# Where the per-layer input p is turned and split: in the expert stage's two ends, or during the input projection

## The chip, the core and the metric

The kernel runs on one core of a Trainium2 chip. The metric is device time in microseconds (us) for one launch, and the number to compare is the median of several launches. One further launch is recorded by the hardware profiler; its rows are what the text below rests on. The engines are PE (TensorE, matrix products and its weight loads PEld), DVE (VectorE), ACT (ScalarE), POOL (GpSimd) and SP (SyncE, which here only issues transfers). Each engine works through its own list of instructions in order, and waits at the head of the list for what the instruction needs.

## What is computed

The reference is a transformer-like encoder layer on 2048 tokens of width 1024, in f32. Cut to what matters here:

```
x   = layernorm(x)
z   = x @ w_in + b_in                      # 1024 -> 2048, then short convolutions and pooling
x   = layernorm(alpha * x + mix(z) @ w_o)
ffn = top-2 experts of 32 (SwiGLU, 1024 -> 512 -> 1024), weighted and summed per token
ple = sigmoid(x @ w_ple_gate + b) * (p @ w_ple_proj)     # p: 2048 x 256
out = layernorm(alpha * x + ffn + ple)
```

The `ple` line is called the embedding below. `p` is an input of 2048 rows by 256; nothing that is computed changes it.

## The kernel before

Products in f32 are made from two halves: a value is split into a high part (a rounding copy on ACT, line 304) and a low part (the difference, on DVE, line 305), and `mm3` (lines 219 to 221) adds high by high, high by low and low by high, each a 128x512 matrix product. An operand whose rows are tokens is first turned on PE (four or eight 128x128 products with the identity into PSUM) and then split out of PSUM.

On-chip memory is handed out in slots by the program as it is written: `FB` holds split operands (26 slots of 128x1024, 12 more before the expert stage), `RB` raw data (9 slots, 12 more from the expert stage on), `ZB` small tiles, `PS` the eight PSUM banks. `Slots.get` takes the slot that has been free longest, and `wait(slots, keep=k)` lets a background job step aside until k more than it needs are free. A background job is a generator that a main loop advances a step at a time (`start(name, gen, rate)`, `run`, `bg.step`). From the program so written a planner orders each engine's list once, when the kernel is built; the transfers that SP issues are in one such list, those of ACT and POOL in the lists of these engines.

The stages, with their times in the profile:

- Up to about 405 us, the input projection: two sweeps `s` over half of the tokens, four column groups `j`, two chunks `c` of 512 tokens (`unit`, 96 products of 128x512 each). Beside it run jobs that load and split the next weights, that rewrite the normalised input (`again`), and, from unit (1, 3, 3) on, `load_wo`, which loads and splits `w_o` (loads at line 596). From unit (1, 0, 3) on one RB slot of zeros is also stored to the unused rows of `yd` from POOL (line 653).
- To about 606 us, the output projection, layer norm and router (`wo_tiles`, `post`, `router`).
- To about 725 us, the embedding of tiles 10 to 15 (`PRE`, `embed`), with the routing beside it; then a loop for overflowing experts (line 1524).
- To about 1452 us, the experts (`stage1`, `stage2`, `hidden`; lines 1403 and 1404 are products for half blocks). Their results are stored to `yd`.
- To the end, the embedding of tiles 0 to 9 (`END`, `embed_tile`), while `finish` and `finish_last` gather each token's two expert rows from `yd` on POOL (line 1616), add them on DVE (lines 1653, 1630), normalise (ACT 1661 and 1667, POOL 1659 to 1669, DVE 1668), and store.

`p` enters only in the embedding. Two tiles at a time, `fetch_p` (line 1092) has SP load 256 rows into half an RB slot, and `load_p` turns them with four PE products (line 1125) into a PSUM bank and splits them into one FB slot, high parts in its first half and low parts in its second. There are eight such pairs: three in `PRE` and five in `END`. `embed_product` takes its left operands from that slot. `prepare` and `prepare_tile` start these jobs one or two tiles ahead, and `start_fetch` loads the first three pairs of `END` early and reserves the RB slots for it (`rclaims`).

In `embed_tile` the sums of the large product leave PSUM by DVE (line 1231, twice for each tile), ACT makes the tanh (1232), and DVE multiplies by the p product (1236).

Of the kernel before, what the change touches and what calls it, by code (L numbers as in the profile page):

```python
# [8 lines left out]
F32 = mybir.dt.float32  # L9
F32R = mybir.dt.float32r  # L10
# [6 lines left out]
N = 2048  # L17
D = 1024
KD = D // 128
NT = N // 128  # L20
# [151 lines left out]
def wait(slots, m=1, align=1, keep=0, late=False):  # L172
    n = 0
    while len(slots.age) < m + keep or not slots.has(m, align, late):
        n += 1
        assert n < 10000, "no slot"
        yield
# [3 lines left out]
def hybrid_conv_pool_hmoe_encoder(ctx, tc, x, p, ln0_g, ln0_b, w_in, b_in, conv_w, pool_w, pool_scale,  # L181
                                  w_o, ln1_g, ln1_b, w_rg, b_rg, w_re, b_re, w1, w3, w2, w_pg, b_pg,
                                  w_pp, ln2_g, ln2_b, out):
    nc = tc.nc
# [3 lines left out]
    FB, RB = Parts(), Parts()  # L188
# [6 lines left out]
    PS = psum.tile([128, 8, 512], F32, name="PS")  # L195
    SF, SR, SZ, SP = Slots(NF, NY), Slots(NR), Slots(NZ), Slots(8)

    def dram(name, shape):
        return nc.dram_tensor(name, shape, F32, kind="Internal").ap()
# [3 lines left out]
    x1d = dram("x1d", (N, D))  # L203
    x1Td = dram("x1Td", (len(END), 2, 128, 1024))
    yd = dram("yd", ((NB + NOV) * 128, D))

    def flat(ap, *shape):
        step, dims = 1, []
        for s in reversed(shape):
            dims.insert(0, [step, s])  # L210
            step *= s
        return bass.AP(tensor=ap.tensor, offset=ap.offset, ap=dims)
# [14 lines left out]
    ident = consts.tile([128, 128], F32, name="ident")  # L227
# [17 lines left out]
    for g in range(4):  # L245
        w = 2 << g
        l, r = w // 2, w // 2 - 1
# [12 lines left out]
    def run(gen):  # L260
        for _ in gen:
            bg.step()

    def after(n, gen):
        for _ in range(n):
            yield
        yield from gen
# [3 lines left out]
    def start(name, gen, rate):  # L271
        jobs[name] = gen
        bg.add(gen, rate)

    def need(name):

        if name in jobs:
            gen = jobs.pop(name)
            n = 0
            while next(gen, DONE) is not DONE:  # L280
                n += 1
                if n > 40:
                    bg.step()
            bg.forget(gen)
# [18 lines left out]
    def split(hi, lo, src, eng=nc.vector):  # L303
        nc.scalar.copy(hi, src)  # L304
        eng.tensor_sub(lo, src, hi)  # L305
# [75 lines left out]
    def again():  # L381

        gr0.append(SR.get())
        gr0.append(SR.get())
        nc.scalar.dma_start(RB[:, gr0[0]], bcast(ln0_g, D))
        nc.scalar.dma_start(RB[:, gr0[1]], bcast(ln0_b, D))
        for t in range(AGAIN):
            yield from wait(SR, keep=2)
            r = SR.get()
            nc.sync.dma_start(RB[:, r], xf[t * 128:(t + 1) * 128, :])  # L390
            yield
            v = RB[:, r]
            s = ln_stats(v)
            yield
            ln_apply(v, s, RB[:, gr0[0]], RB[:, gr0[1]])
            nc.gpsimd.dma_start(x0d[t * 128:(t + 1) * 128, :], v)
            SR.free(r)
            yield
# [21 lines left out]
    def load_w(s, j):  # L420

        for i in range(4):
            if (s, j, i) not in raw:
                yield from wait(SR)
                fetch_w(s, j, i)
                yield
            yield from wait(SF)
            hi = SF.get()
            yield from wait(SF)
            lo = SF.get()  # L430
            r = raw.pop((s, j, i))
            split(FB[:, hi], FB[:, lo], RB[:, r])
            SR.free(r)
            wz[s, j, i] = (hi, lo)
            yield
# [115 lines left out]
    b = SP.get()  # L551
# [20 lines left out]
    def load_wo():  # L572
# [44 lines left out]
        SF.free(ph)  # L617
        SF.free(pl)

    zero_rows = list(range(HROW + HCUM[NE] * 64, (NB + NOV) * 128, 128))  # L620
    for s in range(2):
        for j in range(4):
            for c in (2 * s, 2 * s + 1):
                if (s, j, c) == (0, 0, 0):
                    start("x1", prep(1), 0.8)
                if (s, j, c) == (0, 1, 0):
                    start("again", again(), 0.3)
                    start("x2", prep(2), 0.4)
                if (s, j, c) == (0, 3, 1):
                    start("x3", prep(3), 0.6)  # L630
                if (s, j, c) != (0, 0, 0):
                    need(f"x{c}")
                    need(f"w{s}{j}")
                if (s, j, c) == (1, 3, 2):
                    SF.limit = NF
                if (s, j, c) == (1, 0, 3):
                    need("again")
                    for q in gr0:
                        SR.free(q)
                    zr = SR.get()  # L640
                    nc.gpsimd.memset(RB[:, zr], 0.0)
                if c == 2 * s + 1:
                    if (s, j) == (1, 3):
                        start("wo", load_wo(), 0.75)
                    else:
                        nj = (s, j + 1) if j < 3 else (s + 1, 0)
                        start("w%d%d" % nj, after(9, load_w(*nj)), 0.75)
                run(unit(s, j, c))
                if s and j + c >= 3 and j < 3:
                    for _ in range(-(-len(zero_rows) // (8 - 2 * j - c))):  # L650
                        a = zero_rows.pop(0)
                        e = min(a + 128, (NB + NOV) * 128)
                        tc.keep_in_program_order(nc.gpsimd.dma_start(yd[a:e], RB[:e - a, zr]))
                if j == 3:
                    SF.free(xT[c][0], 4)
                    SF.free(xT[c][1], 4)
# [11 lines left out]
    v = RB[:, wrr, :KD * 36].rearrange("p (k e) -> p k e", e=36)  # L668
# [338 lines left out]


    w1f, w3f, w2f = flat(w1, NE, D, 512), flat(w3, NE, D, 512), flat(w2, NE, 512, D)
    wpg, wpp, pf = flat(w_pg, D, D), flat(w_pp, 256, D), flat(p, N, 256)  # L1010
    wt = {}
    raws = deque()

# [46 lines left out]
    claims, rclaims = [0], [0]  # L1060
    rkeep, routed = [3], []

    def claimed(n):
        yield from wait(SF, keep=n - 1)
        claims[0] -= n
        return [SF.get() for _ in range(n)]
# [18 lines left out]


    based = dram("based", (N, D))
    base, xs, pT, praw = {}, {}, {}, {}

    def fetch_p(ts):  # L1090
        praw[ts[0]] = SR.get()
        nc.sync.dma_start(RB[:, praw[ts[0]], :512].rearrange("p (q c) -> p q c", c=256),
                          pf[ts[0] * 128:(ts[1] + 1) * 128, :].rearrange("(q p) c -> p q c", p=128))

    def fetch_x1(t):
        base[t] = SR.get()
        nc.sync.dma_start(RB[:, base[t]], x1d[t * 128:(t + 1) * 128, :])

    def fetch_embed(ts):
        for i, t in enumerate(ts):  # L1100
            yield from wait(SR)
            rclaims[0] -= 1
            fetch_x1(t)
            if i % 2 == 0:
                yield from wait(SR)
                rclaims[0] -= 1
                fetch_p(ts[i:i + 2])
            yield

    def start_fetch(ts):  # L1110
        rclaims[0] += len(ts) + (len(ts) + 1) // 2
        start(f"fetch{ts[0]}", fetch_embed(ts), 1.0)

    def load_p(ts):

        if ts[0] not in praw:
            yield from wait(SR)
            fetch_p(ts)
            for _ in range(6):
                yield  # L1120
        r = praw.pop(ts[0])
        yield from wait(SP)
        b = SP.get()
        for k in range(4):
            nc.tensor.transpose(PS[:, b, k * 128:(k + 1) * 128], RB[:, r, k * 128:(k + 1) * 128], ident)
        SR.free(r)
        yield
        q, = yield from claimed(1)
        split(FB[:, q, :512], FB[:, q, 512:], PS[:, b])
        SP.free(b)  # L1130
        for i, t in enumerate(ts):
            pT[t] = (q, 2 * i)
        yield
# [14 lines left out]
    def prepare(ts):  # L1148
        for i in range(0, len(ts), 2):
            claims[0] += 1  # L1150
            start(f"p{ts[i]}", load_p(ts[i:i + 2]), 1.0)
        rclaims[0] += sum(t not in base for t in ts)
        start(f"x{ts[0]}", (v for t in ts for v in load_x1(t, False)), 1.0)
# [109 lines left out]
    for ts in groups:  # L1263
# [9 lines left out]
        c, q = divmod(ts[-1], 4)  # L1273
# [250 lines left out]
    with tc.For_i(0, nov_n, 1) as it:  # L1524
# [5 lines left out]
        b = SP.get()  # L1530
        for q in range(2 * NT):
            i, t = divmod(q, NT)
            v = ZB[:, z, (q % 4) * 128:(q % 4) * 128 + 128]
# [49 lines left out]
    def prepare_tile(i):  # L1583
        if i < len(END):
            t = END[i]
            if i % 2 == 0:
                claims[0] += 1
                start(f"p{t}", load_p(END[i:i + 2]), 1.0)
            claims[0] += 2
            start(f"x{t}", load_x1(t, True), 1.0)  # L1590

    start_fetch(END[:6])
    bg.step()
    claims[0] -= 3
# [128 lines left out]
```

## Time and profile before

| | us |
|---|---|
| three launches | 1624.75, 1619.27, 1623.60 |
| their median | 1623.6 |
| profiled execution, as a launch is timed | 1621.81 |
| its span in the profile | 1620.2 |
| mean granted TensorE clock in it | 0.988 of full speed |

The profile's page lists for each engine how long it was busy, and the same in 40 slices of the span. Its views are the groups of instructions by line, what each engine waited for, the instructions in order of time, the sums over chosen stretches, and the chain of waits followed back from the last instruction. A time in brackets behind an instruction is how long its engine had been idle, and the arrow names what ended that. L1125 is line 1125 of the kernel before.

### The profile page before, as it was taken

Reading aid. Unit: us, or ns where it says so; the run is one execution under the profiler, and the core shown is the slowest. Engines: PE = TensorE matmul, PEld = TensorE weight load, DVE = VectorE, ACT = ScalarE, POOL = GpSimd, SP = SyncE. Lnnn points to the kernel's source line nnn. Section 1 sums busy time; section 2 is a strip of 40 time slices with the busy share of each in tenths; the row PEclk is TensorE's granted clock in tenths of the full one; section 3 lists DMA queues with packets and bytes.
Section 4 is the critical chain, followed back from the end, with each engine's and each line's share of the span. In section 5 each row is a group of like instructions: output and inputs, shape, how many; then the busy total and the mean of one; then the engine's idle time right before and its main releaser. Section 6 shows DMA issues by size and latency. Waiting matters only on the chain.

```text
span 1620.2 us, 21581 instructions
## 1 busy us (share of the span) xinstructions
PE 1569.1 (97%) x7371; PEld 1291.6 (80%) x7371; DVE 1157.8 (71%) x1406; ACT 792.0 (49%) x940; POOL 478.3 (30%) x626
## 2 busy tenths in 40 slices
PE   6999999999999998999999999999999999999986
PEld 5887878887888887778888888888888888888865
DVE  7777574345566767768888788777888767776887
ACT  7343342113111124147777767776777657662342
POOL 3454262443233225010202121111212101006874
PEclk9999999999999999999999999999999999999988
DMA  6546168865376536369898998998898987998971
GB/s 209 182 162 214 65 205 276 305 252 161 122 255 205 174 126 253 120 236 383 315 373 314 362 350 309 355 358 330 328 360 302 355 279 274 362 331 332 340 265 65
DMA packets 204809, 427.88 MB, mean 264 GB/s; under 512 B 18856, under 2 KB 70616, under 8 KB 204696
## 3 DMA queue, kind: packets, MB, share of 16 engines
q1 hardware_dynamic: 162096, 292.33, 51.7%
q0 software_dynamic: 34080, 122.96, 20.5%
q10 hardware_dynamic: 8520, 11.18, 2.1%
q8 instruction: 59, 0.97, 0.2%
q14 instruction: 54, 0.44, 0.1%
HBM read 333.10 MB, written 93.32 MB: 263 GB/s over the span
## 4 chain that ended last, share of the span: by engine, by line
PE 37%; issue 11%; POOL 5%; DVE 1%; ACT 1%; DMA 0%; POOLq 0%; DVEq 0%; ACTq 0%
PE PS L219 9%; PE PS L221 9%; PE PS L220 9%; PE PS L1403 3%; PE PS L1404 3%; PE PS L311 2%; POOL RY L1616 1%; PE PS L1461 1%; DMA yd<-RB 0%; POOL RB L1616 0%; DVE RB L1653 0%; POOL RY L1669 0%; POOL rstd L1664 0%; PE PS L1331 0%; POOL nbias L1659 0%
## 5 line engine op out<-in xcount | busy, mean ns | idle before, releaser
L220 PE MATMUL PS<-FB 128*128 128x512 f32 (+1 forms) x1516 | 589.7, 389 | 5.0 <-DVE FB L305 5.0
L219 PE MATMUL PS<-FB 128*128 128x512 f32 (+1 forms) x1436 | 559.9, 391 | 11.6 <-DVE FB L305 7.0
L221 PE MATMUL PS<-FB 128*128 128x512 f32 (+1 forms) x1436 | 557.6, 389 | 1.8 <-DVE FB L305 1.8
L220 PEld LDWEIGHTS PS<-FB 128*128 128x128 f32 x1516 | 287.6, 190 | 61.5 <-DVE FB L305 5.7
L219 PEld LDWEIGHTS PS<-FB 128*128 128x128 f32 x1436 | 272.3, 190 | 66.9 <-DVE FB L305 7.9
L305 DVE TENSOR_TENSOR FB<-RY,FB 128x1024 fp32r<-128x1024 f32 x232 | 281.1, 1230 | 52.1 <-ACT FB L304 29.7
L221 PEld LDWEIGHTS PS<-FB 128*128 128x128 f32 x1436 | 272.0, 189 | 56.6 <-DVE FB L305 2.2
L305 DVE TENSOR_TENSOR FB<-RB,FB 128x1024 fp32r<-128x1024 f32 x212 | 257.5, 1228 | 79.0 <-ACT FB L304 67.3
L304 ACT CAST FB<-RB 128x1024 fp32r<-128x1024 f32 x216 | 223.7, 1050 | 148.5 <-PE PS L220 49.8
L304 ACT CAST FB<-RY 128x1024 fp32r<-128x1024 f32 x236 | 243.1, 1049 | 92.7 <-PE PS L220 27.0
L1316 POOL DMA_INDIRECT RY<-x1d,TBI x29 | 56.5, 1947 | 391.6 <-DVE FB L305 232.0
L305 DVE TENSOR_TENSOR FB<-PS,FB 128x1024 fp32r<-128x1024 f32 (+1 forms) x116 | 103.2, 898 | 68.5 <-ACT FB L304 68.3
L304 ACT CAST FB<-PS 128x1024 fp32r<-128x1024 f32 (+1 forms) x116 | 86.3, 758 | 115.8 <-PE PS L311 77.1
L220 PE MATMUL PS<-FB,FY 128*128 128x512 f32 x264 | 104.2, 395 | 0.0
L1403 PE MATMUL PS<-FB 128*128 128x512 f32 x264 | 103.8, 393 | 0.0
L1404 PE MATMUL PS<-FB 128*128 128x512 f32 x264 | 103.3, 391 | 0.0
L219 PE MATMUL PS<-FB,FY 128*128 128x512 f32 x216 | 86.0, 398 | 0.0
L221 PE MATMUL PS<-FB,FY 128*128 128x512 f32 x216 | 85.5, 396 | 0.0
L219 PE MATMUL PS<-FY,FB 128*128 128x512 f32 x180 | 71.9, 399 | 0.0
L221 PE MATMUL PS<-FY,FB 128*128 128x512 f32 x180 | 70.7, 394 | 0.0
L296 POOL TENSOR_SCALAR rstd<-mv 128x1 f32<-128x1 f32 x42 | 29.3, 700 | 137.2 <-DVE mv L291 124.3
L304 ACT CAST FY<-RB 128x1024 fp32r<-128x1024 f32 (+1 forms) x30 | 31.0, 1036 | 78.8 <-PE PS L220 59.8
(276 smaller groups left out, 2007.6 us busy)
## 6 DMA issues: line engine op xcount, KB each, us to landing
RY<-in_w_dram SPq DMA_DIRECT2D x224, 512.0 KB
RB<-in_w_dram SPq DMA_DIRECT2D x160, 512.0 KB
yd<-RB POOLq DMA_DIRECT2D x59, 512.0 KB
RB<-in_w_in_dram SPq DMA_DIRECT2D x32, 512.0 KB
RB<-in_x_dram SPq DMA_DIRECT2D x24, 512.0 KB
yd<-RY POOLq DMA_DIRECT2D x23, 512.0 KB
x1Td<-FB POOLq DMA_DIRECT2D x20, 512.0 KB
FB<-x1Td SPq DMA_DIRECT2D x20, 512.0 KB
```

The costliest lines, as they stand in the source:

```text
L219: nc.tensor.matmul(o, ah, bh, start=start, stop=False)
L220: nc.tensor.matmul(o, ah, bl, start=False, stop=False)
L221: nc.tensor.matmul(o, al, bh, start=False, stop=stop)
L296: nc.gpsimd.tensor_scalar(rstd[:, s:s + 1], mv[:, s, 1:2], EPS, None, op0=OP.add)
L304: nc.scalar.copy(hi, src)
L305: eng.tensor_sub(lo, src, hi)
L311: nc.tensor.transpose(v[:, k], src[:, k * 128:(k + 1) * 128], ident)
L1316: nc.gpsimd.indirect_dma_start(out=RB[0:64 if half else 128, rows[n]], out_offset=None, in_=x1d, in_offset=bass.IndirectOffsetOnAxis(ap=id ...
L1403: nc.tensor.matmul(o, xs[0][:, c], wh, start=start, stop=False)
L1404: nc.tensor.matmul(o, xs[0][:, c], wl, start=False, stop=stop)
L1461: nc.tensor.transpose(v[:, k], g[:, k * 128:(k + 1) * 128], ident[0:m, 0:m])
L1616: nc.gpsimd.indirect_dma_start(out=RB[:, yq[t, i]], out_offset=None, in_=yd, in_offset=bass.IndirectOffsetOnAxis(ap=SLI[:, i, t:t + 1], ax ...
```

## The change

A new job `turn_p` makes all eight pairs during the input projection: it loads 256 rows of `p`, turns them on PE, splits them into an RB slot, and stores that slot to a new array `pTd` in HBM, from ACT's queue. It is started at unit (1, 1, 2) with 0.6 steps for each step of the main loop. `load_p` becomes one load of 128x1024 from `pTd` straight into the FB slot. `fetch_p` and its RB slots go.

```diff
+    pTd = dram("pTd", (NT // 2, 128, 1024))
...
+    def turn_p():
+
+        pf = flat(p, N, 256)
+        for i in range(NT // 2):
+            yield from wait(SR, keep=3)
+            r = SR.get()
+            nc.sync.dma_start(RB[:, r, :512].rearrange("p (q c) -> p q c", c=256),
+                              pf[i * 256:(i + 1) * 256, :].rearrange("(q p) c -> p q c", p=128))
+            for _ in range(6):
+                yield
+            yield from wait(SP, keep=2)
+            b = SP.get()
+            for k in range(4):
+                nc.tensor.transpose(PS[:, b, k * 128:(k + 1) * 128], RB[:, r, k * 128:(k + 1) * 128], ident)
+            SR.free(r)
+            yield
+            yield from wait(SR, keep=2)
+            r = SR.get()
+            v = RB[:, r].bitcast(F32R)
+            split(v[:, :512], v[:, 512:], PS[:, b])
+            SP.free(b)
+            nc.scalar.dma_start(pTd[i], RB[:, r])
+            SR.free(r)
+            yield
...
+                if (s, j, c) == (1, 1, 2):
+                    start("p", turn_p(), 0.6)
...
     def fetch_embed(ts):
-        for i, t in enumerate(ts):
+        for t in ts:
             yield from wait(SR)
             rclaims[0] -= 1
             fetch_x1(t)
-            if i % 2 == 0:
-                yield from wait(SR)
-                rclaims[0] -= 1
-                fetch_p(ts[i:i + 2])
             yield
 
     def start_fetch(ts):
-        rclaims[0] += len(ts) + (len(ts) + 1) // 2
+        rclaims[0] += len(ts)
...
     def load_p(ts):
 
-        if ts[0] not in praw:
-            yield from wait(SR)
-            fetch_p(ts)
-            for _ in range(6):
-                yield
-        r = praw.pop(ts[0])
-        yield from wait(SP)
-        b = SP.get()
-        for k in range(4):
-            nc.tensor.transpose(PS[:, b, k * 128:(k + 1) * 128], RB[:, r, k * 128:(k + 1) * 128], ident)
-        SR.free(r)
-        yield
         q, = yield from claimed(1)
-        split(FB[:, q, :512], FB[:, q, 512:], PS[:, b])
-        SP.free(b)
+        nc.sync.dma_start(FB[:, q].bitcast(F32), pTd[ts[0] // 2])
```

## Rows read from the trace of the kernel before

**Rows 1.** The page: busy us of each engine; GB/s in 40 slices of 40.5 us.

```profile
PE 1569.1 (97%) x7371; PEld 1291.6 (80%) x7371; DVE 1157.8 (71%) x1406; ACT 792.0 (49%) x940; POOL 478.3 (30%) x626
...
GB/s 209 182 162 214 65 205 276 305 252 161 122 255 205 174 126 253 120 236 383 315 373 314 362 350 309 355 358 330 328 360 302 355 279 274 362 331 332 340 265 65
```

**Rows 2.** Stretches: length; busy PE, PEld, DVE, ACT, POOL; granted clock, DMA share, GB/s.

```profile
243.00:405.00 162.00, 160.66 (x700) 130.67 (x699) 71.40 (x94) 36.70 (x49) 63.53 (x151) 1.00 0.73 249
606.00:725.00 119.00, 111.02 (x545) 89.61 (x543) 85.05 (x147) 38.28 (x48) 29.29 (x20) 0.97 0.58 204
1469.90:1571.30 101.40, 94.70 (x412) 77.77 (x411) 85.32 (x94) 38.24 (x52) 87.26 (x84) 0.95 0.87 315
1540.90:1547.60 6.70, 0.04 (x1) 0.00 (x0) 5.94 (x7) 5.19 (x7) 6.30 (x8) 0.66 0.31 100
1547.60:1605.60 58.00, 57.88 (x244) 47.24 (x244) 49.02 (x56) 20.61 (x27) 36.40 (x34) 0.95 0.56 201
1563.50:1584.00 20.50, 20.50 (x93) 16.87 (x93) 20.08 (x24) 6.47 (x11) 7.67 (x9) 1.00 0.65 226
```

**Rows 3.** PE in order of time: three instructions that ended an idle time.

```profile
399.02 0.73 PE L219 MATMUL PS<-FY 128*128 128x512 f32 x2 [1.34 <-ACT FY L304]
...
634.40 0.50 PE L220 MATMUL PS<-FB 128*128 128x512 f32 x1 [3.68 <-DVE FB L305]
...
1547.64 0.80 PE L219 MATMUL PS<-FB 128*128 128x512 f32 x1 [6.70 <-DVE FB L305]
```

**Rows 4.** All PE products of line 1125: ns min/median/max, first and last start.

```profile
L1125 PE MATMUL PS<-ident,RY x24: 271/272/328, 656.8 to 1569.2; 128*128 128x128 f32 x24
...
L1125 PE MATMUL PS<-ident,RB x8: 270/272/307, 606.7 to 656.7; 128*128 128x128 f32 x8
```

**Rows 5.** PE in order of time around the first turned pair: start, us.

```profile
606.71 0.60 PE L1125 MATMUL PS<-ident,RB 128*128 128x128 f32 x4
607.06 0.48 PE L219 MATMUL PS<-FB 128*128 128x512 f32 x1
607.37 0.40 PE L220 MATMUL PS<-FB 128*128 128x512 f32 x1
```

**Rows 6.** PE in order of time where the last expert ends.

```profile
1450.39 0.60 PE L1125 MATMUL PS<-ident,RY 128*128 128x128 f32 x4
1450.82 0.60 PE L1461 MATMUL PS<-ident,ZB 128*128 128x128 f32 x4
1451.65 0.65 PE L1125 MATMUL PS<-ident,RY 128*128 128x128 f32 x4 [0.23 <-ACT RY L1503]
1452.63 0.50 PE L219 MATMUL PS<-FB 128*128 128x512 f32 x1 [0.32 <-ACT FB L304]
```

**Rows 7.** ACT in order of time: two casts there, and one activation near the end.

```profile
1451.50 1.08 ACT L304 CAST FB<-PS 128x512 fp32r<-128x512 f32 x2
...
1550.22 1.24 ACT L1667 ACTIVATE RB<-RB,nbias,rstd 128x1024 f32<-128x1024 f32 x1 [4.10 <-POOL nbias L1665]
```

**Rows 8.** SP's queue in order of time: six loads of w_o.

```profile
251.63 38.67 SPq L596 DMA_DIRECT2D RB<-in_w_o_dram  x6
```

**Rows 9.** The chain of waits in order of time: the last expert store landing.

```profile
1461.11 8.06 DMA yd<-RB
```

**Rows 10.** DVE in order of time near the end.

```profile
1546.89 0.69 DVE L305 TENSOR_TENSOR FB<-PS,FB 128x512 fp32r<-128x512 f32 x1
1551.49 3.40 DVE L1668 TENSOR_TENSOR RB<-RB,RY 128x1024 f32<-128x1024 f32 x1 [3.91 <-ACT RB L1667]
1554.81 1.27 DVE L1231 TENSOR_TENSOR ZB<-PS,RB 128x512 f32<-128x512 f32 x2
...
1591.35 1.27 DVE L1231 TENSOR_TENSOR ZB<-PS,RB 128x512 f32<-128x512 f32 x2
...
1603.46 1.28 DVE L1231 TENSOR_TENSOR ZB<-PS,RB 128x512 f32<-128x512 f32 x2
```

**Rows 11.** PE in order of time: its last product.

```profile
1605.12 0.39 PE L221 MATMUL PS<-FB 128*128 128x512 f32 x1
```

More of the change, by code (lines that the diff above doesn't have):

```diff
@@ L1009, in hybrid_conv_pool_hmoe_encoder @@
     w1f, w3f, w2f = flat(w1, NE, D, 512), flat(w3, NE, D, 512), flat(w2, NE, 512, D)
-    wpg, wpp, pf = flat(w_pg, D, D), flat(w_pp, 256, D), flat(p, N, 256)
+    wpg, wpp = flat(w_pg, D, D), flat(w_pp, 256, D)
     wt = {}
@@ L1087, in hybrid_conv_pool_hmoe_encoder @@
     based = dram("based", (N, D))
[L1088 to L1093, printed above, removed]
+    base, xs, pT = {}, {}, {}
     def fetch_x1(t):
```

## The prediction

> **What bounds the kernel now.** I read the page first: PE is busy 97% of the span, DVE 71%, ACT 49% [rows 1]. PE busy is no proof that PE sets the end, so I took the sums over those stretches that the change touches [rows 2]. In the input projection, from 243 to 405 us, PE has 160.66 of 162.00 us, DVE 71.40 and ACT 36.70: PE sets the pace and both others have room. From 606 to 725 us, where the first three pairs of p are used, PE has 8 us of gaps. At the end it is different. From 1469.9 to 1571.3 us POOL is busy 87.26 of 101.40 us with gathers and additions, and from 1563.5 to 1584.0 us DVE is busy 20.08 of 20.50. The third view, PE in order of time, shows three gaps that matter [rows 3]: 1.34 us before the output projection (a cast of `w_o`), 3.68 at 634 (a weight's low part), and 6.70 at 1547.64, which the split of p for tiles 6 and 7 ends. That last wait is the only stall that p causes openly. About 240 products, four tiles' worth, follow it (244 instructions to 1605.6 us, [rows 2]), so PE stood before tile 6's large product, which does not read p: it waited for the PSUM bank that p's split still held.
>
> **The sum, against the profiled execution's own 1621.8 us** (span 1620.2 and 1.6 around it; the median of the launches is 1623.6, 1.8 higher, and their spread is 5.5).
>
> Eight groups of four turns come into the projection. There are 32 now, one instruction 271 to 274 ns in the two rows' medians, but pipelined [rows 4]. From 606.71 to 607.37 PE did four turns and one product [rows 5]; a product costs 0.23 (607.06 would have been followed at 607.29), so a group costs 0.43 us. Eight cost 3.4. From below: if they fill the stretch's 1.34 us of gaps, 2.1. From above, with an empty pipeline on both sides, as at 1451.65 to 1452.63 [rows 6], 0.98 each, 7.8. I take 3.4, since the projection has a product waiting on both sides. **+3.4**
>
> Three groups leave the stretch from 606 to 725, where PE is busy 111 of 119 us: 3 x 0.43. At worst they filled gaps and nothing is gained; if gaps shrink with them, more (a rival below). **-1.3**
>
> Two groups leave the end of the last expert. There, four turns of p stand ahead of the expert's own turns, and the four behind them stand where PE waits for a cast anyway [rows 6]. ACT does two casts in a row, 1.08 us, one of them p's [rows 7]; without it the expert's own cast ends 0.54 earlier and PE goes on at 1452.1. Bounds 0 and 1.1. **-0.5** This also brings the last store to `yd` forward, whose landing (8.06 us, [rows 9]) releases the gathers; two of three loads of p now come after it, and the first has 512 KB for 256, so that landing has 256 KB less beside it. I count that as nothing; both ways it is under a microsecond.
>
> Three groups leave the tail, and with them their splits. I take nothing for PE there, and this is the step on which the forecast hangs. The 6.70 us are spent while POOL works 6.30 of them [rows 2]. After the gap, DVE's order shows who is late: the addition that empties tile 5's banks ran only at 1554.81, because DVE stood 3.91 us before it for an activation which had itself waited 4.10 us for POOL, and then took 3.40 over line 1668 [rows 7, 10]. Line 1231 for tile 8 ran at 1591.35, though PE ran four tiles in 58 us and so had ended that tile's large product near 1589; for tile 9 it ran at 1603.46, 1605.5 less the last 12 products of 0.23 being 1602.7 [rows 10, 11]. So DVE reaches each tile after PE is done. If PE comes 6.70 us earlier, and 2.9 more for the clock (granted 0.95 over 58 us; PE runs at the 1.2 GHz level after the gap) [rows 2], it only waits longer for banks. What moves the end is DVE's own list: one p split of 0.69 us lies in its full stretch after 1563. **-0.7** Bounds: 0 (the room goes into a wait for POOL) and -9.6 (the whole stall and its clock).
>
> DVE and ACT get eight splits in the projection, 8 x 0.69 and 8 x 0.54 us, 5.5 and 4.3 [rows 7, 10]. They lie beside products: DVE is idle 90.6 us there and ACT 125.3 [rows 2]. The store is issued on ACT's queue and waits for DVE's difference; behind it ACT's next copies out of PSUM stand. PE takes one bank for about 5.5 us of products (24 of 0.23) and has eight, so a delay of several us reaches nobody. Cost 0; without that cover 8 x 1.23, 9.8.
>
> Transfers: 2.1 MB of loads and 4.2 MB of stores come into the projection, and 2.1 MB more are loaded later. 162 us at 249 GB/s are 40 MB [rows 2]; slices of up to 383 GB/s occur [rows 1], so 62 MB would fit, and 46.6 are wanted. Cost 0; without room, 6.3 MB at 383 GB/s, 16 us. The Trainium skill ("DMA: Bandwidth & Descriptors", section "Issuing engines are not separate DMA queues") speaks against the idea that a store from ACT's queue is free: transfers issued by SP, ACT and POOL run on the same DMA engines and interleave. Its section "Anatomy of one DMA" gives a fixed 2.0 us and then 436 GB/s; by that estimate sixteen transfers need 46 us if they follow one another, against none in my sum. The trace of before has none of these transfers, and cannot decide.
>
> SP: the loads of p wait for RB slots, and what is queued behind them are the loads of `w_o`, six of which now go out from 251.63 to 290.3 [rows 8]. The new job takes its slots first. It has 8 to 9 steps a pair, 72 in all, at 0.6 a step: 120 of the 192 steps of its six units, some 83 of 132 us, so from about 273 to 356. That leaves 43 us before the 399 at which `w_o` is wanted. Cost 0 (price below). In the tail, SP's load of a p pair replaces one that waited for an RB slot; it needs an FB slot that one tile before has freed, and is wanted a tile, 13.6 us, later. Cost 0; if one is late, PE has the 6.70 us it used to stand. In RB, three early slots come free, which may let weights or gathers go out sooner; I count nothing.
>
> Sum: 3.4 - 1.3 - 0.5 - 0.7 = +0.9: 1622.7 in terms of the profile, 1624.5 in terms of the median. Between the two I forecast **1623 us**, no change that can be told: a measurement of this kernel tells about 0.3%, 4.9 us.
>
> **Rivals.**
>
> *PE leads the tail after all.* The stall and its slow clock go, 9.6 us instead of 0.7: 1622.7 - 8.9 = 1613.8. For it: PE has 57.88 busy of 58.00 us after the stall, and the planner may draw DVE's list differently once p is out of it. Against it: DVE's additions behind PE at tiles 5, 8 and 9. It decides if the changed kernel's last product comes at 1596 and the end follows.
>
> *Weights come sooner in the first embedding.* An RB slot fewer is held at 600 us, the weight late at 634 is loaded earlier, and 3.68 us of gap go with some 1.5 of slow clock behind it: 1622.7 - 5.2 = 1617.5. For it: loads there go out as RB slots come free. Against: one slot of 21, held briefly.
>
> *`w_o` comes late (slower).* Its loads stand behind p's, the RB slots come back only when the stores of p have landed, and zeros are stored to `yd` in bursts beside it. A load of 512 KB among others lands after about 8 us, as the store to `yd` did [rows 9]; one load late makes the 1.34 us gap 9.4: 1622.7 + 8 = 1630.7. It decides once p's job ends after about 385 us (399 less the landing and a split) instead of 356. For it: from 251 to 356 us three queues would be at work at once, in a stretch that moves 249 GB/s already [rows 2]. Against: 43 us of room. (The rule of the Trainium skill named above, in "DMA: Bandwidth & Descriptors", section "Issuing engines are not separate DMA queues", would bring it about.)
>
> *It does not do what it says.* p is kept in HBM, so a load and a wait for it stay; the stall moves from the split to the transfer. Then the tail is as before: 1623.4, inside the forecast.
>
> **Chances.** The forecast 0.52 (the last rival in it), PE in the tail 0.20, weights 0.08, `w_o` late 0.17, other shifts of the planner's order 0.03. The forecast's own range is 1619 to 1628. Faster by over 0.3%: 0.20 and most of 0.08; slower: 0.17 and a little. The range of 1612 to 1630 takes in the PE case whole and leaves out most of the slow one, and of the bounds above all but those in which several covers fail together.
>
> **What would show it.** In the projection, 32 turns between 270 and 360 us at 0.43 a group, no new gap of PE there and none over 2 us at its end. Between 1540 and 1548 the PE gap gone or moved, the last product before 1600, and still line 1231 of the last tile after it by some us: PE early and DVE, ACT and POOL not. I am wrong if the end follows PE, or if PE stands for `w_o` or for a bank of the new job.

## The result: 14 us slower, most of it made in the last stage

Six launches of the changed kernel have a median of 1637.3 us (1635.3 to 1640.6) against 1623.4 before; the medians lie 13.9 us apart. The ratio, which the text goes by from here on, is 1.0090 with a 95% interval of 1.0079 to 1.0102, some 14.6 us. The forecast was 1623 in 1612 to 1630. The profiled execution spans 1633.7 us, 13.5 more than before.

The page of the changed kernel (answers to [rows 1]): every engine is as busy as before, to within 2.4 us. What was added is waiting.

```profile
PE 1571.0 (96%) x7370; PEld 1294.0 (79%) x7371; DVE 1160.0 (71%) x1406; ACT 791.9 (48%) x940; POOL 476.1 (29%) x626
```

PE in order of time in the changed kernel (answers to [rows 3, 6, 11]; lines past the change are 1 to 28 higher). The wait before the output projection is as it was, only 2.44 us later. At the last expert's end (1454.28 to 1456.27) it takes 1.99 us where before took 2.48 (1450.15 to 1452.63; the row by itself below is before's). The wait of 6.70 us at 1547.64 is gone, but one of 7.69 has come at 1578.57, for DVE's multiplication by a tile's p product (line 1242, before 1236), which frees that product's bank, and no longer for p's split. PE ends 2.6 us later than before, the kernel 13.5.

```profile
401.46 0.73 PE L220 MATMUL PS<-FY 128*128 128x512 f32 x2 [1.34 <-ACT FY L305]
...
622.91 0.50 PE L792 MATMUL PS<-FB 128*128 128x512 f32 x1 [2.03 <-ACT FB L305]
...
1454.28 0.39 PE L222 MATMUL PS<-FB 128*128 128x512 f32 x1
...
1456.27 0.50 PE L220 MATMUL PS<-FB 128*128 128x512 f32 x1 [1.15 <-ACT FB L305]
...
1578.57 0.79 PE L220 MATMUL PS<-FB 128*128 128x512 f32 x1 [7.69 <-DVE ZB L1242]
...
1607.75 0.39 PE L222 MATMUL PS<-FB 128*128 128x512 f32 x1
```

```profile
1450.15 0.40 PE L221 MATMUL PS<-FB 128*128 128x512 f32 x1
```

DVE in order of time in the changed kernel, and one row of the kernel before (answers to [rows 10]; line 1237 empties a tile's banks, 1674 is the scaling of a finished tile, line 1668 before). Tile 0's banks are emptied at 1473.82, tile 9's at 1616.95: 143.1 us. Before, the same two rows stand at 1471.37 and 1603.46: 132.1 us. I call this stretch the tail; it grew by 11.0 us. Tile 8's addition at 1607.25 stands behind a scaling that waited 2.55 us for ACT.

```profile
1473.82 1.37 DVE L1237 TENSOR_TENSOR ZB<-PS,RB 128x512 f32<-128x512 f32 x2 [10.82 <-PE PS L222]
...
1606.11 1.23 DVE L1674 TENSOR_TENSOR RB<-RB 128x1024 f32<-128x1024 f32 x1 [2.55 <-ACT RB L1673]
1607.25 1.28 DVE L1237 TENSOR_TENSOR ZB<-PS,RB 128x512 f32<-128x512 f32 x2
...
1616.95 1.28 DVE L1237 TENSOR_TENSOR ZB<-PS,RB 128x512 f32<-128x512 f32 x2
```

```profile
1471.37 1.37 DVE L1231 TENSOR_TENSOR ZB<-PS,RB 128x512 f32<-128x512 f32 x2 [10.60 <-PE PS L221]
```

What the 11.0 us are made of can be read from the sums over the two tails (columns as in [rows 2]), first before, then the changed kernel:

```profile
1471.36:1603.46 132.10, 125.40 (x547) 103.17 (x546) 114.33 (x129) 47.87 (x65) 102.56 (x100) 0.96 0.75 271
```

```profile
1473.82:1616.95 143.13, 126.63 (x548) 103.86 (x546) 111.34 (x124) 46.44 (x62) 101.62 (x101) 0.95 0.71 261
```

DVE works 3.0 us less and stands idle 14.0 us more (31.8 for 17.8). What DVE waited for in the tail, us in total, times and longest, before and then in the changed kernel: its scaling stood for ACT's normalising of the same tile 12.9 us in nine places before, 25.9 in twelve now.

```profile
DVE RB L1668 <- ACT RB L1667: 10.6, 6, 3.9
DVE RY L1668 <- ACT RY L1667: 2.3, 3, 1.4
```

```profile
DVE RY L1674 <- ACT RY L1673: 13.5, 6, 4.8
DVE RB L1674 <- ACT RB L1673: 12.4, 6, 4.0
```

So most of the tail's loss is one wait, repeated: DVE comes to a tile's scaling before POOL and ACT have finished their part of that tile.

When tile 0 to 9's banks were emptied (first half), from the same view of three kernels:

```
before  1471.4 1483.6 1502.7 1515.5 1533.7 1554.8 1567.0 1575.4 1591.3 1603.5
e1      1474.1 1487.3 1506.3 1519.1 1537.1 1558.2 1570.4 1578.8 1595.3 1607.4
after   1473.8 1486.0 1505.9 1521.0 1535.6 1553.8 1573.3 1590.9 1607.2 1617.0
```

e1 (below) keeps before's order and runs 2.7 to 4.0 us behind it throughout. The changed kernel is up to 5.5 us behind before until tile 3, 1.0 ahead at tile 5, and 15.5 behind at tile 7.

### The profile page after: what moved, and what is told of

The parts are those of the page before. It is cut to its first block, busy times and chain, and to the rows that moved or that the text cites. A ratio compares the mean times of both kernels' runs of the same rounds, so it can differ in the third digit from the quotient of the medians.

```text
span 1633.7 us, 21592 instructions
## 1 busy us (share of the span) xinstructions
PE 1571.0 (96%) x7370; PEld 1294.0 (79%) x7371; DVE 1160.0 (71%) x1406; ACT 791.9 (48%) x940; POOL 476.1 (29%) x626
## 5 line engine op out<-in xcount | busy, mean ns | idle before, releaser
L306 DVE TENSOR_TENSOR FB<-RY,FB 128x1024 fp32r<-128x1024 f32 x238 | 284.6, 1219 | 65.3 <-ACT FB L305 38.7
L306 DVE TENSOR_TENSOR FB<-RB,FB 128x1024 fp32r<-128x1024 f32 x206 | 249.6, 1226 | 95.5 <-ACT FB L305 83.4
L305 ACT CAST FB<-RY 128x1024 fp32r<-128x1024 f32 x243 | 249.5, 1049 | 104.6 <-PE PS L221 29.7
L305 ACT CAST FB<-RB 128x1024 fp32r<-128x1024 f32 x209 | 216.3, 1050 | 168.3 <-DMA RB<-in_w_in_dram 59.2
L306 DVE TENSOR_TENSOR FB<-PS,FB 128x1024 fp32r<-128x1024 f32 (+2 forms) x108 | 98.0, 915 | 66.8 <-ACT FB L305 66.6
L305 ACT CAST FB<-PS 128x1024 fp32r<-128x1024 f32 (+2 forms) x108 | 81.9, 772 | 100.3 <-PE PS L312 78.6
L1322 POOL DMA_INDIRECT RB<-x1d,TBI x14 | 29.7, 2120 | 176.3 <-DVE FB L306 123.6
L220 PE MATMUL PS<-FY,FB 128*128 128x512 f32 x180 | 72.2, 401 | 0.0
```

Of the source, the lines that this page charges most:

```text
L220: nc.tensor.matmul(o, ah, bh, start=start, stop=False)
L1322: nc.gpsimd.indirect_dma_start(out=RB[0:64 if half else 128, rows[n]], out_offset=None, in_=x1d, in_offset=bass.IndirectOffsetOnAxis(ap=id ...
```

## The experiments

Ratios are to the kernel before, timed on the same chip; 0.001 is 1.6 us. "Tail" is the stretch above, from one profile each; where two kernels have the same lists in it (before and e1, after and e2, e5 and e6) it agrees to 1.6 us.

| run | what | ratio, 95% interval | tail, us |
|---|---|---|---|
| before | | 1 | 132.1 |
| after | the change | 1.0090 (1.0079 to 1.0102) | 143.1 |
| e1 | p turned and stored in the projection, not used | 1.0022 (1.0010 to 1.0033) | 133.3 |
| e2 | stored parts used in the last stage alone | 1.0081 (1.0066 to 1.0095) | 144.5 |
| e4 | after, PSUM banks go round as before | 1.0068 (1.0051 to 1.0084) | 143.1 |
| e6 | after, RB slots go round as before | 1.0077 (1.0062 to 1.0092) | 138.0 |
| e5 | after, both as before | 1.0053 (1.0036 to 1.0070) | 136.5 |
| f3 | e5 with before's lists in the tail | 1.0031 (1.0017 to 1.0044) | 133.9 |
| f1 | after with before's lists | 1.0118 (1.0099 to 1.0137) | 150.0 |
| f2 | before with after's lists | 1.0230 (1.0212 to 1.0249) | 172.9 |
| n1 | after, one RB slot held | 1.0031 (1.0021 to 1.0041) | 137.6 |
| n2 | before, one RB slot held | 1.0097 (1.0082 to 1.0111) | 148.8 |
| n3 | before, one bank passed over once | 1.0038 (1.0024 to 1.0052) | 138.1 |
| n4 | after, three RB slots passed over once | 1.0069 (1.0053 to 1.0085) | 144.9 |
| s1 | after, squares moved ahead | 1.0096 (1.0080 to 1.0111) | 148.1 |
| s2 | before, squares moved ahead | 1.0017 (1.0004 to 1.0029) | 134.9 |
| s3 | n1, squares moved ahead | 1.0059 (1.0045 to 1.0073) | 141.9 |
| s4 | after, tiles 7 and 8 emptied sooner | 1.0102 (1.0084 to 1.0121) | 148.6 |
| s6 | after, tile 8 emptied sooner | 1.0097 (1.0077 to 1.0116) | 144.6 |
| s5 | before, tile 7 emptied later | 1.0008 (0.9996 to 1.0020) | 135.5 |

**Which part of the change.** My theory was that the tail's lists come out in another order; the rivals were the projection's extra work, the transfers of p in the tail, and the banks.

e1: `turn_p` is added to the kernel before and nothing else.

> All eight pairs of p are turned, split and stored during the projection as in the changed kernel, but nobody loads the stored parts: both places that use p still load, turn and split it themselves, in the slots and banks of the kernel before. What the projection costs alone. If the loss is made in the tail by what replaces p's turns there, only the projection's own cost is left: 1626 to 1627 us (before's 1623.4 plus the 2.4 us by which the gap ahead of the output projection came later, up to the 3.4 of the forecast). If the loss is made by the extra work of the projection and by everything coming later, it is all here: 1635 to 1638. If the tail is so touchy that any shift reorders it, the time lies anywhere from 1618 to 1638, and the gap ahead of the output projection still stands near 401.5.

The cost of the projection alone. PE over the stretch from the turn that waits near 222 us to the wait for `w_o`, first before, then e1 (columns as in [rows 2]):

```profile
222.05:399.00 176.95, 175.59 (x769) 143.06 (x769) 79.57 (x100) 46.27 (x64) 75.98 (x160) 1.00 0.73 248
```

```profile
221.88:402.36 180.48, 179.14 (x801) 146.16 (x801) 83.93 (x108) 50.16 (x72) 70.58 (x160) 1.00 0.78 281
```

32 products more, 3.55 us of PE more, 3.53 us longer: nothing else in the projection paid. The same stretch is 176.9 us in n2 and n3 and 180.5 in the changed kernel, e4, e6, f1 and f3. The tail keeps its order and, to 1.2 us, its length. The rest of the loss is elsewhere.

e2: `load_p` takes the stored parts for tiles 0 to 9 only.

```diff
+        if ts[0] in END:
+            q, = yield from claimed(1)
+            nc.sync.dma_start(FB[:, q].bitcast(F32), pTd[ts[0] // 2])
```

> Half of the change: p is turned and stored in the projection, the last stage loads the stored parts as in the changed kernel, but the first three pairs are still loaded, turned and split where they are used. If the loss is made in the tail, it is here: 1634 to 1638, the last gather near 1578 and the end as after. If it comes from the first embedding (3.68 us of stalls there turned into many small ones) or is passed on from there, 1624 to 1628.

As expected of the tail: it holds the loss.

**Transfers, slots or banks.** In e5, e4 and e6 the loads of p stay; what before held for p is taken and given back unused.

```diff
+        praw[ts[0]] = SR.get()      # e5, e6: the RB slot, with before's waits
...
+        yield from wait(SP)         # e5, e4: the bank (e4 for tiles 0 to 9 alone)
+        b = SP.get()
         nc.sync.dma_start(FB[:, q].bitcast(F32), pTd[ts[0] // 2])
+        SP.free(b)
```

> As the changed kernel, the stored parts are loaded everywhere and no p is turned or split after the projection. But each load of p takes, holds and gives back the SBUF slot and the PSUM bank that the kernel before used for turning it, without using them. So the rotation of slots and banks in the tail, and with it the order of claims, is that of the kernel before. If the loss comes from the rotation (which bank or slot the next tile gets), the tail is as quick as before and the time is 1622 to 1627. If it comes from the transfers themselves (512 KB a pair on SP's queue in the tail, and waits for them), the loss stays: 1634 to 1638.

> The changed kernel with one thing put back for the five pairs of p used in the last stage: a PSUM bank is taken before the load and given back after it, without use. The large products then go round three pairs of banks with a fixed fourth between them (6, 4, 2, 4, 0, 4, ...) as before, in place of two that alternate (6, 2, 6, 2, ...). SBUF slots of the gathers stay as in the changed kernel. If the alternation of two pairs is what makes the tail late, 1624 to 1628. If it is the SBUF slots of the gathers, or the transfers of p, 1634 to 1638.

> As e5, but only the SBUF slot that p had before is taken and given back, not the PSUM bank: the large products of the last stage alternate between two pairs of banks as in the changed kernel. The engines' lists come out in the same order as in e5. If banks cost nothing, the time is e5's, 1630 to 1634, some 4 us under the changed kernel, and the SBUF slots are what sets the changed kernel apart from e5. If the alternation costs the 3.4 us that e4 gained, 1634 to 1638.

e5 falls between its two cases. By the tail's lengths the RB slots count: with before's slots 136.5 and 138.0, with the new ones 143.1 in both. The banks move the tail by 0 to 1.6 us; e6's surplus over e5 lies rather in the first embedding, where 336.5 us pass from the wait for `w_o` to the wait near 730, against 331.3 in e5. By the medians alone slots and banks can't be told apart, and e5's profiled launch was 4.2 us quicker than its median (1628.15 against 1632.37), so that its tail may be shorter than usual.

**The order alone.** f3, f1 and f2 fix the order in which DVE, ACT and POOL issue the last stage, from the order in another kernel, by edges that order and don't wait. In f1 and f2 that holds for POOL's arithmetic only; the planner places its gathers.

```diff
+    ORDERS["DVE"] = [0, 1, 2, 5, 10, 3, 7,
...
+    for a, b in zip(order, order[1:]):
+        tc.add_manual_dep(chain[b], chain[a].name, no_sync)
```

> The same as e5 (stored parts loaded everywhere, p's SBUF slots and banks taken and given back without use), but VectorE, ScalarE and GpSimd are made to issue the last stage's instructions in the order in which the kernel before issues them, gathers and stores included. Only p's own turns and splits are missing from it. If e5's 9.7 us over before beyond the projection's 3.5 come from the order into which the planner puts the three engines' lists once p's instructions are gone, they vanish: 1623 to 1627 us. If they come from the loads of the stored parts (waits for 512 KB, contention), they stay: 1630 to 1634.

f3 loads the stored parts, and its time cannot be told from e1's (1.5 us more, give or take 3). So the transfers of p cost nothing that can be told here. The order costs the 3.6 us by which f3 lies below e5, but only just: the intervals of the two overlap. f3 also settles what PE's stall was worth. PE in f3: its one wait over 0.3 us in the tail is 1.66 us, and it ends at 1603.35.

```profile
1562.60 0.50 PE L220 MATMUL PS<-FB 128*128 128x512 f32 x1 [1.66 <-DVE ZB L1256]
...
1603.35 0.39 PE L222 MATMUL PS<-FB 128*128 128x512 f32 x1
```

PE in e1, which still turns p there:

```profile
1551.01 0.80 PE L220 MATMUL PS<-FB 128*128 128x512 f32 x1 [7.35 <-DVE FB L306]
...
1608.14 0.39 PE L222 MATMUL PS<-FB 128*128 128x512 f32 x1
```

f3's PE ends 4.8 us sooner although its tail began 1.9 us later (tile 0's banks at 1475.97 and 1474.08), and its tail is no shorter: DVE empties tile 9's banks at 1609.87, 6.5 us after PE's last product began, in e1 at 1607.42, before it.

> The changed kernel with its own slots and banks, but VectorE's and ScalarE's lists of the last stage, and GpSimd's arithmetic in it, in the order of the kernel before; the gathers on GpSimd stay where the planner puts them, since the new SBUF slots forbid the old place of some. If the order of the arithmetic makes the loss, most of the 10.5 us made in the tail come back: 1626 to 1630. If the slots make it (a gather that waits for a slot delays every tile, whatever the order of the rest), 1634 to 1640.

> The converse: the kernel before, with no work added anywhere and with p turned and split where it was, but VectorE's and ScalarE's lists of the last stage, and GpSimd's arithmetic in it, in the order of the changed kernel. If the order makes the loss, it appears without any part of the change: 1630 to 1636. If slots or transfers make it, 1621 to 1625.

f1's expectation by the order fell: over the new slots the old order is no better than the planner's own, rather worse. f2's direction came, at 37 us three times the most that was expected, and more than twice what the change itself loses: in its trace DVE waits 33.9 us in six places for gathers, in before's 0.2 in one. An order is good only over the slots that it was made for. POOL's whole old order over the new slots was not tried: some gather would stand ahead of what frees its slot.

**Is it the change, or any disturbance?** Each of these adds the lines shown at the start of the last stage.

```diff
+    SR.get()                        # n1 to after, n2 to before
...
+    SP.free(SP.get())               # n3, to before
...
+    for _ in range(3):              # n4, to after
+        SR.free(SR.get())
```

> The changed kernel with one SBUF slot of RB taken out of use for the whole last stage, nothing else: the slot that p's raw tiles had needed before and that the change set free. The three engines' lists then come out much nearer to those of the kernel before. If the slot set free is what turns the lists to the worse, 1628 to 1633, 4 to 9 us under the changed kernel. If a slot more can only help, or does nothing, 1636 to 1642.

> The kernel before with one SBUF slot of RB taken out of use for the last stage, nothing else. The lists of the three engines come out far from before's, about as far as the changed kernel's. If before's lists are one good draw among many, and a disturbance of any kind loses it, 1629 to 1640 with no work added. If one slot more is what hurts, one slot fewer does not: 1620 to 1627.

> The kernel before with the next PSUM bank taken and given back once at the start of the last stage, so that the banks come round in another order; nothing else. A small disturbance: the lists change in few places. If any disturbance loses before's time, 1627 to 1635; if before's time does not hang on the draw, 1620 to 1627.

> The changed kernel with three SBUF slots of RB taken and given back once at the start of the last stage, so that the gathers get other slots in turn; nothing else. If the tail's time is a draw, it may come out anywhere from 1626 to 1645, more than 4 us from the changed kernel's 1637 on either side as likely as not. If the loss is the change's own (transfers, banks, one free slot), 1634 to 1640.

n2 and n3 add no work and lose 15.8 and 6.2 us. n1 takes a slot away from the changed kernel and gets 9.6 us back; what is left, 5.0, can't be told from e1's 3.6, though its one profiled tail is still 4.3 us longer than e1's. DVE in n1, tile 0 and tile 9:

```profile
1472.47 0.69 DVE L1237 TENSOR_TENSOR ZB<-PS,RB 128x512 f32<-128x512 f32 x1 [10.83 <-PE PS L222]
...
1610.09 1.28 DVE L1237 TENSOR_TENSOR ZB<-PS,RB 128x512 f32<-128x512 f32 x2
```

So the tail's length hangs on how slots and lists happen to come out. Of the eight orders that the planner made itself (e1 has before's, e2 the changed kernel's, e6 has e5's), before's gives the shortest tail. n4 moved less than I thought likely.

**Which place in the lists.** In the changed kernel ACT has each tile's square behind the normalising of the tile before (from tile 2 to 4), where before has two squares together. s1 to s3 move `sq` of six, four and five tiles ahead in the forced lists, and the scaling of the mean on POOL with it.

> The changed kernel with its own lists on VectorE, ScalarE and GpSimd, but for six tiles the square (ScalarE) stands in front of the normalising of the tile before, and the scaling of the mean that it needs (GpSimd) in front of that tile's power. So two tiles' chains can run at once. In the changed kernel's profile the scaling starts 3.3, 4.8 and 6.3 us after the sum that it needs in three of these places. If one chain at a time is what makes its lists slow, 1626 to 1633. If it is something else in the lists (the additions that empty the banks behind the sums, the gathers), 1634 to 1640.

> The kernel before with the same rule on its own lists, which finds four such places. If the chains bound it as well, 1617 to 1622; if its lists already run two chains at a time where it matters, 1622 to 1627; if a square put ahead waits for a late gather and holds the normalising up, over 1627.

> The changed kernel with one SBUF slot held in the last stage (n1) and the same rule on its lists, which finds five places. If the chains bound it, 1622 to 1627; if not, 1627 to 1632 as n1.

This theory fell: no tail got shorter; they are 5.0, 2.8 and 4.3 us longer than those of after, before and n1. The second place was DVE's emptying of the banks of tiles 7 and 8 (below, `ev` empties, `pr` takes the product, `sum` adds the expert rows, `mul` scales; not all entries are shown):

```diff
-... mul.5 sum.6 ev.7 pr.7 mul.6 sum.7 mul.7 ev.8
+... ev.7 mul.5 sum.6 pr.7 mul.6 sum.7 ev.8 mul.7      # s4; s6 has ev.8 alone
```

> The changed kernel with its own lists, but VectorE's additions that empty the banks of tile 7 stand ahead of the scaling of tile 5 instead of five operations behind it, and those of tile 8 ahead of tile 8's and 7's finishing; ScalarE's tanh of both move with them. In the changed kernel's profile tile 7's banks are emptied at 1590.9 and tile 8's at 1607.2, against 1575.4 and 1591.3 before. If this place costs the time, the tail gets some 5 to 10 us shorter: 1627 to 1632. If not, 1635 to 1640.

> The changed kernel with its own lists, but only tile 8's additions (and tanh) are moved ahead of the last finishing steps of tiles 8 and 7. In the changed kernel's profile they wait some 5 us behind tile 7's scaling (1602.3 to 1607.2). If that wait is on the path alone, 1631 to 1634; if tile 7's place decides, 1635 to 1639.

> The converse on the kernel before: tile 7's additions, products' sums and tanh stand behind the scaling of tile 5, as in the changed kernel; nothing else is changed. In before's profile that scaling ran at 1584.1 and the additions at 1575.4. If this place costs the time, 1629 to 1635; if not, 1621 to 1626.

It fell too. In s4 tile 7's banks and in s6 tile 8's are emptied sooner after tile 0's (by 8 and 5 us), and neither kernel gains. s5 emptied tile 7's banks at 1584.6 in place of 1575.4; its one profiled tail is 3.4 us longer, but its time can't be told from before's (1.3 us more, at most 3.2). Forcing lists as such costs no more than that, then. None of the three places that I moved carries the loss; which places do, alone or together, stays open. No version beat the kernel before: f3 shows that even with before's order the change has nothing to win.

## Why the prediction was wrong

By its own terms, each from the profiles:

| step | predicted | measured |
|---|---|---|
| eight groups into the projection (e1) | +3.4 | +3.53 |
| three groups out of 606 to 725 | -1.3 | +1.85 (one execution of each) |
| two groups at the last expert's end | -0.5 | -0.49 |
| the tail | -0.7 | +11.0 |

They add up to 15.9; of the 2.4 us to the spans' 13.5, 1.1 is a shorter start of this execution (401.46 less 180.48 is 220.98 us, before 222.05 up to that stretch), and 1.2 lies between the last expert's cast and tile 0's emptying (18.7 us before, 17.6 now). The last gain is no accident, since n1, s1, s4 and s6 have 17.6 too, and f2, n2, s2 and s5 18.7; its cause was not followed up.

**The projection** was right: 0.44 us a group. The turns ran from 267.1 to 335.6 us and the last store of p landed at 352.7, near the 273 to 356 of the prediction. Two of its figures are off without harm: both medians of [rows 4] are 272 ns, and 399 less a landing of 8.06 and a split of 1.23 is 389.7 us, not 385. `w_o` was not late (1.34 us, as before), so the rival with the right sign had the wrong place. The transfers that were priced at nothing cost nothing: e1's stretch moves 281 GB/s for 248. The rule of the Trainium skill that the prediction weighed ("DMA: Bandwidth & Descriptors", section "Issuing engines are not separate DMA queues") would have them interleave with the rest, which they may do; no wait of PE shows it. The prediction's estimate of 46 us takes figures that the Trainium skill (the same page, section "Anatomy of one DMA — SWDGE (gpsimd) path") gives for transfers issued by GpSimd, while those of p go out from SP and ACT; the four stores of p whose landing the changed kernel's trace shows took 3.8 to 8.3 us each.

**The first embedding.** The -1.3 did not come. The 3.68 us at 634 went, and with it one of 2.87 at 650 (for the routing) that the prediction did not name; eight waits of 0.45 to 2.03 us came between 620 and 691 (one stands above), for casts and differences of weights and for the routing. Up to the wait near 730 (726.83 and 731.12) PE's waits add up to the same, 9.8 us before and 9.7 now, and the clock granted over the last 121 and 123 us of it is 0.97 before and 0.94 now. The +1.85, from 327.8 us between the wait for `w_o` and the wait near 730 to 329.7, is one execution of each and mostly chance: kernels with the same instructions as before up to there (before, f2, n2, n3, s2, s5) take 327.8 to 330.4 us, 328.9 in the mean, and those with the changed kernel's (after, e4, f1, n1, n4, s1, s3, s4, s6) 328.8 to 329.7, 329.2 in the mean. So nothing was gained, and no loss can be told. "At worst they filled gaps and nothing is gained" is what happened.

**The last expert** was right to 0.01 us: ACT has one cast there in place of two (1455.62 to 1456.21 us), and all nine kernels that have the changed kernel's instructions up to there show this 1.98 to 1.99. n3 gets the same with p still turned there: its two casts, 1453.74 to 1454.82, let PE go on after the first, at 1454.38.

**The tail.** "The step on which the forecast hangs", that PE's 6.70 us are worth nothing there, was right: f3 shows it, and "What moves the end is DVE's own list" was right too. What failed is the -0.7, which took that list as given less one split, and the sentence "In RB, three early slots come free, which may let weights or gathers go out sooner; I count nothing", and the 0.03 for "other shifts of the planner's order". I read in the profile that DVE, ACT and POOL set the tail's end, and then took their lists as given while the change altered what they are made from: which slot each gather gets, and which instructions stand between. In place of 0.7 us less, the tail took 11.0 more: DVE's 3.0 us less of work were real, but its waits grew by 14.0, 13.0 of them for the normalising on ACT. By the ratios, taking p out with slots and banks kept costs 5.0 us beyond the projection (e5 less e1), of which f3 gives 3.6 back; the new slots and banks make the other 6.0 (after less e5), and one slot held gives 9.6 of all this back. The intervals of such differences are 2.5 to 3.5 us either way, so how much falls to the lists and how much to the slots is known only roughly. That lists and slots can make such a loss is clear: n2, n3 and f2 lose 6 to 37 us without any part of the change.

## What to carry to other kernels

Where three engines hand each tile on and a planner writes their lists, price the lists first: hold one slot or pass one bank over in the kernel before and time it. If that alone moves the time by more than the change should, a forecast by instructions saved has no meaning there, and the change is to be judged with the order held (e5 and f3) before it is judged as it comes out. A stall of the busiest engine is worth nothing in a stage whose end other engines set; look at who ends last after the stall.

## What the hardware showed beside it

An addition of DVE with two inputs in SBUF (1.28 us) took 3.41 when POOL's addition had started before it. DVE, then POOL, in the changed kernel:

```profile
1585.14 3.41 DVE L1636 SCALAR_TENSOR_TENSOR RB<-RY,GW,RB 128x1024 f32<-128x1024 f32 x1
...
1589.69 1.28 DVE L1636 SCALAR_TENSOR_TENSOR RB<-RY,GW,RB 128x1024 f32<-128x1024 f32 x1
```

```profile
1584.11 3.37 POOL L1675 TENSOR_TENSOR RY<-RY 128x1024 f32<-128x1024 f32 x1 [2.61 <-DVE RY L1674]
```

DVE ended 1.07 us after POOL (1588.55 and 1587.48), about its own length: it had waited for POOL, and not shared. POOL's addition, 2.4 us otherwise, took 3.37 behind an addition of DVE that had started 0.16 us before it (1583.95). The Trainium skill ("SBUF — State Buffer", section "Who interferes with whom") says that a DVE instruction with two SBUF inputs contends with a GpSimd instruction that reads SBUF, and that the later one blocks until the first is done; the rows agree, to some 0.2 us. It is one way in which the order of two lists becomes time, but it does not make the tail's 11 us: from tile 0's emptying on, eight DVE instructions of over 1.9 us overlap such an addition of POOL in each kernel, together 22.2 us before and 22.1 in the changed kernel.

The start of the kernel varies by itself: the turn that waits near 222 us came at 221.0 to 225.3 us in the sixteen profiles that show it, those of kernels with and without the change mixed. That may be a good part of the 5 us by which launches of one kernel differ; no launch but the profiled one shows its parts.
